# Sums over a head's features: one product with a block-diagonal matrix in place of sums by token, a copy and transposes

## The chip, the cores and the metric

The kernel runs on one core of a Trainium2 chip, as one launch. The time is device microseconds of that core; of the kernel before, three runs are shown. The core has five engines with a program each: TensorE (PE, its weight loads shown as PEld), the vector engine (DVE), the scalar engine (ACT), GpSimd (POOL) and SyncE (SP, which issues the DMAs). They meet at semaphores only.

## What is computed

One inference step through two layers of a hybrid backbone, for 128 context tokens and 256 latent tokens of 1024 features. Each layer is a half-step gated feed-forward, a mixer, and a second half-step feed-forward, each with a layer norm behind it. The mixer's input projection feeds three branches: windowed attention (A), neighbourhood attention (B) and a bidirectional RWKV-7 recurrence (C); each is projected, gated and merged. The change is in branch C, eight heads of 64 features, in two places:

```python
kk = split_heads((k * lp['k_k']).astype(f32), C_HEADS)
kk = kk / jnp.maximum(jnp.sqrt(jnp.sum(kk * kk, axis=-1, keepdims=True)), 1e-12)
...
mu = y.mean(-1, keepdims=True)
var = jnp.mean(jnp.square(y - mu), -1, keepdims=True)
yn = ((y - mu) * lax.rsqrt(var + GN_EPS)).reshape(B, L, C_WIDTH) * lp['gn_g'] + lp['gn_b']
```

Both are a sum over the 64 features of a head for each token, a root, a reciprocal, and a product with each of the 64 features.

## The kernel before

All activations lie with 128 features on the partitions and the 384 tokens along the free axis; a tile of branch C holds two heads (a pair), on partitions 0 to 63 and 64 to 127. Matrix products are made of three float32r products (lines 387 to 389 and 397 to 399) of a high and a low part of weights and activations. The large weights come as a stream of 512 KB units; ACT writes the high part (hi) and DVE the low part (lo). Instructions of ACT, DVE and POOL are recorded through a helper, so all of theirs carry line 290.

The mixer of a layer (`mixer`, line 844) is an attention stage (`attention`, line 1089) and then a scan stage. In the attention stage, `conv_gen` (line 1254) also makes the projections of branch C that the first pairs need, with a convolution over three neighbouring tokens. For a key tile it squares the keys and, two steps into the next projection, runs `norms` (line 1282): the sums kss, a root, a maximum and a reciprocal into rn.

The scan stage (`rwkv_gen`, line 1367) takes four pairs p = 0 to 3 through `rwkv_prepare` (line 1411; the factors of the recurrence, among them nkk, the negated normed keys), `rwkv_chunks` (line 1484; the inversion of 64 x 64 blocks, which begins with products into lu) and `rwkv_scan` (line 1655; the recurrence, then y's group norm with the products gm and gss, then och and ocl, the two parts of the branch's output). The preparation of pair p + 1 and the scan of pair p - 1 are dealt out among the steps of pair p's inversion. Behind the last pair's scan stand the products of branch C's projection (pp<-och).

A small sum is made by `head_sums` (line 1303): the squares serve as weights, 128 tokens at a time, against a constant "sel" of two columns, so the sums come out with tokens on the partitions, six columns (three blocks of tokens, two heads). To bring the six columns of reciprocals back to features on partitions, `head_spread` (line 1308) copies them into a 128 x 384 tile rb, each repeated 64 times, and transposes it block by block into a PSUM tile "spread".

The order is set by a list scheduler from priorities that the program states (`tc.high_priority`, with offsets by stage), and by `beside` (line 1325): every small product or transpose of a scan that goes through `rmm` or `rtr` (lines 1335 and 1339) adds to a debt, by its size and a rate of the phase, and as long as the debt is positive, steps of dense work are issued behind it. That dense work (`mixer_fill`, line 944) is branch B's gates and projections, the projections of the later pairs and branch C's gates (tile pz); what is left of it comes behind the last scan. PSUM tiles come from pools of 3 buffers (kss, pz, pp, among others) and of 2 buffers (spread, gss, gm, up and others of the scan). A constant "blk", 128 x 128 with ones where two features belong to the same head, is there already, for another sum (bon).

Of the kernel before, what the change touches and what calls it, by code (L numbers as in the profile page):

```python
# [101 lines left out]
def _consts():  # L102
# [15 lines left out]
    add("sel", (p[:, None] // HD == np.arange(2)[None, :]))  # L118
# [73 lines left out]
# sets of four groups of 256 modulations; the first two are what the first chunks of features need, then the others  # L192
# [3 lines left out]
def _layout(inp):  # L196
    """Rearranges the inputs (permutations and concatenations only)."""
# [36 lines left out]
    # [l][d][h = (p, e)][v][k] -> [l][(e, k)][p][d][v]  # L234
# [8 lines left out]
def _weights(inp, order):  # L243
    """The large weights as 128 x 128 blocks in the order of their use."""
# [22 lines left out]
def _unlayout(r):  # L267
# [7 lines left out]
    st = r["o_st"].reshape(DEPTH, 2, HD, 4, 2, HD)  # l, e, k, p, d, v  # L275
# [4 lines left out]
class Engine:  # L280
    """An engine that knows its last instruction."""
# [14 lines left out]
def trunk(tc, I, O, order, taps=None, stop=None):  # L296
# [5 lines left out]
    def then(*engines):  # L302
        """Behind the last instruction so far of these engines."""
        st = ExitStack()
        for e in engines or (V, S, G):
            if e.last is not None:
                st.enter_context(tc.issue_after(e.last.ins))
        return st
# [32 lines left out]
    class Stream:  # L341
# [16 lines left out]
        def ahead(self):  # L358
            """Out of the steady state: the unit after the next is split as soon as the last is used up."""
            if len(self.left) <= UNIT and self.unit < WS_UNITS:  # L360
                self.fetch(self.offset)
# [20 lines left out]
    def mm3(out, chunks, xs, after=()):  # L382
        """out += sum of W_k^T x_k, with both factors as sums of two float32r parts."""
# [7 lines left out]
    def mm3_steps(out, chunks, xs, step=2):  # L391
        """mm3 in steps of a few chunks, with what each costs."""
# [10 lines left out]
    def split(dst_h, dst_l, src, lo_eng):  # L403
        """src (SBUF or PSUM, float32) = dst_h + dst_l."""
# [30 lines left out]
    def ada_beside(pool, n):  # L435
        """The next n steps with the products on the vector engine: where that has time, and the tensor engine has not."""
# [38 lines left out]
    def ada_flush():  # L475
        """To columns: out[feature, (block, group, stream)]."""
# [20 lines left out]
    ax = [act.tile([P, NTOK], F32, name=f"ax{c}") for c in range(KD)]  # L497
    # (four more columns: see Norm)
# [8 lines left out]
    class Norm:  # L507
        """Layer norm over the features of y = alpha x + gate * out, chunk by chunk as out comes.
        The next phase's input is h = rs g1 (y - mu) + b1, g1 and b1 per feature and stream, rs and mu per token. Its
        first products W^T h run on z = g1 y, before rs and mu are known: rs W^T z - rs mu W^T g1 + W^T b1, with g1 and  # L510
        b1 as four more columns of z."""
# [34 lines left out]
        def add(self, c, po):  # L546
# [4 lines left out]
            if c == 0:  # L551
                # the table of Sqrt is there when it is needed
# [27 lines left out]
        def pilot(self):  # L580
            # about the mean of the first four chunks
# [14 lines left out]
        def products(self, chunks, xs, c):  # L596
            """The products of chunk c of out."""
# [14 lines left out]
        def finish(self, head=iter(())):  # L612
            """head: products of the next phase, in steps, from those on z to the last before h is needed."""
# [47 lines left out]
        def h(self, pool, c):  # L661
            """The next phase's input, in two parts."""
# [11 lines left out]
        def x(self):  # L674
            """alpha times the norm's output."""
# [5 lines left out]
    class Head:  # L681
        """The first products of a phase, on z: two groups of them, each chunk by chunk."""
# [1108 lines left out]
```

## Time and profile before

| | |
|---|---|
| median of 3 runs | 2436.55 us (2436.5 to 2436.74) |
| span of the profiled execution | 2439.6 us (the profile gives no other time of that execution) |
| instructions | 42863 |
| PE busy | 2297.4 us, 94% of the span |
| PEld busy | 2106.5 us, 86% |
| DVE busy | 1696.6 us, 70% |
| ACT busy | 1056.4 us, 43% |
| POOL busy | 550.0 us, 23% |
| chain that ended last | PE 71%, DVE 15%, ACT 5%, issue 4%, DMA 3%, POOL 2% |
| mean granted TensorE clock | 0.983 |

The profile is of one execution, by the hardware profiler. Busy time is the union of an engine's instructions; a matmul's end is modelled, so that neighbouring matmuls overlap in it, and what a product costs is read from the distance of the starts. The chain is followed back from the last instruction, at each step to what released it. In the window tables each engine's busy time stands with its count of instructions, and PEclk is the clock that the throttle granted TensorE, as a share of full speed.

### The profile page before, as it was taken

How to read it: one execution, taken by the hardware profiler on the slowest of the kernel's cores; microseconds unless marked ns; L12 is line 12 of the kernel's file. 1: busy time of each engine (PE TensorE's matmuls, PEld its weight loads, DVE VectorE, ACT ScalarE, POOL GpSimd, SP SyncE). 2: the span in 40 equal slices, each digit the busy share in tenths (PEclk: the TensorE clock that was granted, in tenths of full speed). 3: DMA queues.
4: the chain of work that ended last, by engine and by line, in shares of the span. 5: the costliest groups of instructions: out<-in, count | busy, mean ns of one | idle time of the engine just before them, and what ended most of it. 6: DMA issues, size and time to landing. Idle time of an engine off the chain costs nothing.

```text
span 2439.6 us, 42863 instructions
## 1 busy us (share of the span) xinstructions
PE 2297.4 (94%) x17066; PEld 2106.5 (86%) x17066; DVE 1696.6 (70%) x2865; ACT 1056.4 (43%) x1942; POOL 550.0 (23%) x522
## 2 busy tenths in 40 slices
PE   7999999998899998999999999899989999999998
PEld 5999988897777788999889999889877777889997
DVE  3797886777767568786978954776787674665534
ACT  3333245655545445333243332555555454443332
POOL 2111422101122044211432113310022220542113
PEclk9999999999999999999999999999999999999999
DMA  8575644242111262665546743523321113534332
GB/s 314 193 240 198 191 122 130 84 111 78 40 57 47 72 209 95 191 217 180 180 147 205 244 130 122 154 81 91 112 70 39 51 50 90 204 102 140 130 121 87
DMA packets 125079, 324.54 MB, mean 133 GB/s; under 512 B 31568, under 2 KB 50256, under 8 KB 124880
## 3 DMA queue, kind: packets, MB, share of 16 engines
q1 hardware_dynamic: 124880, 321.81, 41.1%
q8 instruction: 134, 2.20, 0.4%
q14 instruction: 65, 0.53, 0.1%
HBM read 312.06 MB, written 9.70 MB: 132 GB/s over the span
## 4 chain that ended last, share of the span: by engine, by line
PE 71%; DVE 15%; ACT 5%; issue 4%; DMA 3%; POOL 2%; SPq 0%; POOLq 0%; ACTq 0%; DVEq 0%
PE po L399 5%; PE po L398 5%; PE po L397 5%; PE pa L387 4%; PE pg L389 4%; PE pa L388 4%; PE pg L387 4%; PE pg L388 4%; PE pa L389 4%; DVE lo L290 3%; DVE acc L290 2%; PE pz L397 2%; DMA adaw<-wada 2%; ACT hi L290 2%; PE pz L398 2%
## 5 line engine op out<-in xcount | busy, mean ns | idle before, releaser
L290 DVE TENSOR_TENSOR lo<-raw,hi 128x1024 fp32r<-128x1024 f32 (+1 forms) x472 | 583.8, 1246 | 305.9 <-ACT hi L290 303.8
L290 ACT ACTIVATE hi<-raw 128x1024 fp32r<-128x1024 f32 x418 | 441.7, 1058 | 785.0 <-issue 267.5
L290 DVE SCALAR_TENSOR_TENSOR acc<-adaw,cs,acc 128x1024 f32<-128x1024 f32 x224 | 292.3, 1327 | 0.0
L290 POOL TENSOR_TENSOR ul<-si,uh 128x384 fp32r<-128x384 f32 x88 | 126.3, 1435 | 579.3 <-ACT uh L290 579.3
L399 PE MATMUL po<-uh,lo 128*128 128x384 f32 x704 | 238.6, 339 | 6.3 <-DVE lo L290 6.3
L397 PE MATMUL po<-uh,hi 128*128 128x384 f32 x704 | 239.7, 340 | 0.0
L398 PE MATMUL po<-ul,hi 128*128 128x384 f32 x704 | 238.0, 338 | 0.0
L387 PE MATMUL pg<-zh,hi 128*128 128x384 f32 x656 | 224.1, 342 | 9.1 <-DVE si L290 9.1
L388 PE MATMUL pg<-zl,hi 128*128 128x384 f32 x656 | 223.8, 341 | 0.0
L389 PE MATMUL pg<-zh,lo 128*128 128x384 f32 x656 | 223.2, 340 | 0.0
L387 PE MATMUL pa<-zh,hi 128*128 128x384 f32 x632 | 216.2, 342 | 4.9 <-ACT si L290 4.4
L389 PE MATMUL pa<-zh,lo 128*128 128x384 f32 x632 | 213.8, 338 | 0.6 <-DVE lo L290 0.6
L388 PE MATMUL pa<-zl,hi 128*128 128x384 f32 x632 | 214.2, 339 | 0.0
L399 PEld LDWEIGHTS po<-uh,lo 128*128 128x128 f32 x704 | 133.5, 190 | 7.3 <-DVE lo L290 7.3
L397 PE MATMUL pz<-zh,hi 128*128 128x384 f32 x352 | 128.1, 364 | 8.5 <-ACT hi L290 5.7
L397 PEld LDWEIGHTS po<-uh,hi 128*128 128x128 f32 x704 | 133.7, 190 | 2.2 <-issue 0.8
L398 PEld LDWEIGHTS po<-ul,hi 128*128 128x128 f32 x704 | 133.5, 190 | 1.4 <-issue 0.8
L387 PEld LDWEIGHTS pg<-zh,hi 128*128 128x128 f32 x656 | 125.0, 191 | 10.0 <-ACT hi L290 6.7
L399 PE MATMUL pz<-zh,lo 128*128 128x384 f32 x352 | 126.3, 359 | 4.1 <-DVE lo L290 4.0
L387 PEld LDWEIGHTS pa<-zh,hi 128*128 128x128 f32 x632 | 119.1, 188 | 9.8 <-ACT si L290 5.3
L389 PEld LDWEIGHTS pg<-zh,lo 128*128 128x128 f32 x656 | 125.6, 191 | 1.6 <-issue 1.6
L388 PEld LDWEIGHTS pg<-zl,hi 128*128 128x128 f32 x656 | 125.0, 191 | 1.6 <-issue 1.6
(390 smaller groups left out, 5157.4 us busy)
## 6 DMA issues: line engine op xcount, KB each, us to landing
raw<-ws SPq DMA_DIRECT2D x418, 512.0 KB, 3.5
adaw<-wada SPq DMA_DIRECT2D x144, 512.0 KB, 4.8
bm<-rpb SPq DMA_DIRECT2D x64, 64.0 KB, 7.1
axd<-ax SPq DMA_DIRECT2D x16, 192.0 KB, 5.2
gcd<-gt SPq DMA_DIRECT2D x16, 192.0 KB, 4.7
gc<-gcd SPq DMA_DIRECT2D x16, 192.0 KB, 3.4
ax<-axd SPq DMA_DIRECT2D x16, 192.0 KB, 4.8
xt<-xt SPq DMA_DIRECT2D x8, 192.0 KB, 8.6
```

The costliest lines, as they stand in the source:

```text
L290: self.last = f(*a, **k)
L387: T.matmul(out, wh, xh, start=(k == 0), stop=False)
L388: T.matmul(out, wh, xl, start=False, stop=False)
L389: T.matmul(out, wl, xh, start=False, stop=(k == n - 1))
L397: T.matmul(out, wh, xh, start=(k == 0), stop=False)
L398: T.matmul(out, wh, xl, start=False, stop=False)
L399: T.matmul(out, wl, xh, start=False, stop=(k == n - 1))
```

## The change

The constant "sel", `head_sums` and `head_spread` go. Each sum is one product of the block-diagonal constant "blk" with the 128 x 384 squares, whose result stands on every feature of the head at once; root and reciprocal run on all of it. For the keys, the minus sign goes into the maximum's instruction, rn is a tile of 128 x 384 (two buffers), and the normed keys are one instruction in its place. For the group norm, root and reciprocal overwrite the tile of the squares (gsq). The sum of the group norm now goes through `rmm`, and the transposes, which went through `rtr`, are gone.

```diff
-    add("sel", (p[:, None] // HD == np.arange(2)[None, :]))
...
                 def norms(p=p, sq=sq):
                     pss = mmp("kss")
-                    head_sums(pss, sq)
-                    w[f"rn{p}"] = rn = keep.tile([P, 6], F32, name=f"rn{p}")
-                    S.activation(out=rn, in_=pss[:, 0:6], func=AF.Sqrt)
-                    V.tensor_scalar(out=rn, in0=rn, scalar1=1e-12, scalar2=None, op0=ALU.max)
+                    T.matmul(pss[:, :NTOK], C("blk"), sq, start=True, stop=True)
+                    w[f"rn{p}"] = rn = keep.tile([P, NTOK], F32, tag="rn", bufs=2, name=f"rn{p}")
+                    S.activation(out=rn, in_=pss[:, :NTOK], func=AF.Sqrt)
+                    V.tensor_scalar(out=rn, in0=rn, scalar1=1e-12, scalar2=-1.0, op0=ALU.max, op1=ALU.mult)
                     V.reciprocal(rn, rn)
...
-    def head_sums(out, sq):
-        for b in range(3):
-            T.matmul(out[:, 2 * b : 2 * b + 2], sq[:, b * P : (b + 1) * P], C("sel"), start=True, stop=True)
-
-    def head_spread(pool, rn):
-        rb = pool.tile([P, 3, 2, HD], F32, tag="rb", bufs=1, name="rb")
-        V.tensor_copy(rb, rn.rearrange("p (b e) -> p b e", e=2).unsqueeze(3).to_broadcast([P, 3, 2, HD]))
-        pe = rwp("spread")
-        for b in range(3):
-            rtr(pe[:, b * P : (b + 1) * P], rb[:, b].rearrange("p e f -> p (e f)"))
-        return pe[:, :NTOK]
...
-        nkk = pool.tile([P, NTOK], F32, tag="nkk", bufs=1, name="nkk")
-        V.tensor_scalar(out=nkk, in0=k, scalar1=vcol(l, "k_k")[:, p : p + 1], scalar2=-1.0, op0=ALU.mult, op1=ALU.mult)
-        V.tensor_tensor(out=nkk, in0=nkk, in1=head_spread(pool, w[f"rn{p}"]), op=ALU.mult)
+        nkk = w[f"rn{p}"]
+        V.scalar_tensor_tensor(out=nkk, in0=k, scalar=vcol(l, "k_k")[:, p : p + 1], in1=nkk, op0=ALU.mult, op1=ALU.mult)
...
         pst = rwp("gss")
-        head_sums(pst, sq)
-        rn = pool.tile([P, 6], F32, tag="grn", bufs=1, name="grn")
-        S.activation(out=rn, in_=pst[:, 0:6], func=AF.Sqrt, bias=C("geps"), scale=1.0 / HD)
-        V.reciprocal(rn, rn)
-        V.tensor_tensor(out=k, in0=k, in1=head_spread(pool, rn), op=ALU.mult)
+        rmm(pst[:, :NTOK], C("blk"), sq, start=True, stop=True)
+        S.activation(out=sq, in_=pst[:, :NTOK], func=AF.Sqrt, bias=C("geps"), scale=1.0 / HD)
+        V.reciprocal(sq, sq)
+        V.tensor_tensor(out=k, in0=k, in1=sq, op=ALU.mult)
```

Since priorities and the debt of dense work set the order, the edit moves other instructions too. The rows below are of the instruction order of the two kernels; the number behind a name tells one buffer's contents from the next, and lines from 290 on are lower in the changed kernel.

The vector engine in the attention stage, at the second kss of the first layer (nm, sm and pe are the softmax's maximum, sum and probabilities; lo the low part of a weight unit; r a projection with its convolution). Before:

```order
L290 TENSOR_REDUCE nm<-sl 128x1 x2
L290 TENSOR_SCALAR nm<-nm 128x2
L290 TENSOR_SCALAR rn_5337<-rn_5337 128x6
L290 RECIPROCAL rn_5337<-rn_5337 128x6
L290 TENSOR_TENSOR lo<-raw,hi 128x512 x2
L290 RECIPROCAL sm<-sm 128x2
L290 TENSOR_SCALAR pe<-pe,sm 128x384 x2
```

Now:

```order
L289 TENSOR_REDUCE nm<-sl 128x1 x2
L289 TENSOR_SCALAR nm<-nm 128x2
L289 TENSOR_SCALAR rn_5333<-rn_5333 128x384
L289 RECIPROCAL rn_5333<-rn_5333 128x384
L289 TENSOR_TENSOR lo<-raw,hi 128x512 x2
L289 RECIPROCAL sm<-sm 128x2
L289 SCALAR_TENSOR_TENSOR r_5379<-pc,vec_108,r_5379 128x127
L289 TENSOR_SCALAR pe<-pe,sm 128x384 x2
```

The wide maximum and reciprocal stand at the place of the narrow ones, ahead of the same softmax, and one product of a convolution has come ahead of the probabilities.

The vector engine at the end of the first layer's last scan (k holds y, gp the norm's gain, gc the gates of branch C). Before:

```order
L290 TENSOR_TENSOR k_6257<-gm,gp 128x384
L290 RECIPROCAL grn<-grn 128x6
L290 COPY rb<-grn 128x384
L290 TENSOR_TENSOR lo<-raw,hi 128x1024
L290 TENSOR_TENSOR k_6257<-k_6257,spread 128x384
L290 SCALAR_TENSOR_TENSOR gc<-gc,pp 128x384 x2
```

Now:

```order
L289 TENSOR_TENSOR k_6245<-gm,gp 128x384
L289 RECIPROCAL gsq<-gsq 128x384
L289 TENSOR_TENSOR lo<-raw,hi 128x512
L289 TENSOR_TENSOR k_6245<-k_6245,gsq 128x384
L289 TENSOR_TENSOR lo<-raw,hi 128x512 x7
L289 TENSOR_TENSOR lo<-raw,hi 128x1024 x2
L289 SCALAR_TENSOR_TENSOR gc<-gc,pp 128x384
```

Copy and spread are gone, and seven and two low parts of weights now stand between the norm's product and the first use of branch C's projection.

TensorE at the same place: the gss of the last pair and what follows it (pz is a gate's product, pp<-och and pp<-ocl branch C's projection). Before:

```order
L1306 MATMUL gss<-con,gsq 128x2 x3
L399 MATMUL pz<-zh_95,lo 128x384
L397 MATMUL pz<-zh_97,hi 128x384
L398 MATMUL pz<-zl_98,hi 128x384
L399 MATMUL pz<-zh_97,lo 128x384
L397 MATMUL pz<-zh_99,hi 128x384
L398 MATMUL pz<-zl_100,hi 128x384
L399 MATMUL pz<-zh_99,lo 128x384
L397 MATMUL pz<-zh_101,hi 128x384
L398 MATMUL pz<-zl_102,hi 128x384
L399 MATMUL pz<-zh_101,lo 128x384
L397 MATMUL pp<-och_6919,hi 128x384
```

Now, the last rows ahead of the first pp<-och:

```order
L396 MATMUL pz<-zh_101,hi 128x384
L397 MATMUL pz<-zl_102,hi 128x384
L398 MATMUL pz<-zh_101,lo 128x384
L396 MATMUL pp<-och_6878,hi 128x384
L397 MATMUL pp<-ocl_6879,hi 128x384
L396 MATMUL pp<-och_6878,hi 128x384
```

Before, 10 dense products stand between the last gss and the first product on och; now 134, all of them gates' products. Counted over the first layer's scan stage, up to the last gss, 125 dense products fewer stand on TensorE. Between the first lu of one pair and of the next there are 20 more (pair 0 to 1), 64 fewer (1 to 2) and 39 fewer (2 to 3), and from there to the last gss 39 fewer. Loads of ACT's function tables in its order are 44 where there were 40.

## Rows read from the trace of the kernel before

**Rows 1.** Windows, first layer's scans: engines' busy time (instructions), clock, DMA share, GB/s

```profile
575.00:890.00 315.00, 291.33 (x3575) 243.17 (x3573) 221.82 (x453) 156.07 (x286) 72.15 (x97) 0.98 0.23 74
```

**Rows 2.** Windows, cut at each pair's first lu and at the last gss

```profile
605.00:659.96 54.96, 48.34 (x712) 40.06 (x712) 40.23 (x78) 30.42 (x59) 12.13 (x20) 0.94 0.12 41
659.96:734.00 74.04, 70.66 (x884) 58.52 (x884) 51.76 (x118) 34.20 (x67) 15.24 (x22) 0.98 0.18 56
734.00:793.90 59.90, 56.85 (x812) 46.15 (x810) 45.22 (x95) 32.35 (x63) 14.95 (x21) 0.97 0.15 48
793.90:866.00 72.10, 66.42 (x894) 55.20 (x893) 41.94 (x99) 33.06 (x59) 6.71 (x7) 1.00 0.23 72
```

**Rows 3.** Windows, 30 us and 5 us of the first pair's section

```profile
600.00:630.00 30.00, 25.79 (x362) 23.15 (x362) 26.42 (x49) 14.55 (x27) 4.04 (x5) 0.90 0.17 54
...
625.00:630.00 5.00, 4.69 (x107) 4.68 (x108) 2.30 (x7) 3.08 (x4) 0.00 (x0) 0.50 0.01 3
```

**Rows 4.** TensorE's waits, 575 to 890 us: total us, times, longest us

```profile
PE spread L1340 <- ACT gp L290: 1.5, 2, 0.8
...
PE pp L398 <- POOL ocl L290: 0.5, 1, 0.5
...
PE pp L397 <- ACT och L290: 0.3, 1, 0.3
```

**Rows 5.** Timeline of TensorE, last pair: start, us, instruction

```profile
864.44 0.83 PE L1306 MATMUL gss<-con,gsq 128*128 128x2 f32 x6
...
867.49 0.34 PE L397 MATMUL pp<-och,hi 128*128 128x384 f32 x1
867.67 0.49 PE L1340 MATMUL spread<-con,rb 128*128 128x128 f32 x3
867.91 0.42 PE L398 MATMUL pp<-ocl,hi 128*128 128x384 f32 x1
868.17 0.34 PE L399 MATMUL pp<-och,lo 128*128 128x384 f32 x1
868.35 0.34 PE L397 MATMUL pp<-och,hi 128*128 128x384 f32 x1
```

**Rows 6.** Timeline of TensorE, bonus sum of the last pair

```profile
799.41 0.81 PE L1336 MATMUL bon<-bo,con 128*128 128x384 f32 x2
```

**Rows 7.** Groups by line and shape, vector engine: reciprocals

```profile
L290 DVE RECIPROCAL sm<-sm 128x2 f32<-128x2 f32 x48 | 7.8, 162 | 15.0 <-ACT pe L290 14.6
...
L290 DVE RECIPROCAL rn<-rn 128x6 f32<-128x6 f32 x8 | 1.5, 188 | 0.2
...
L290 DVE RECIPROCAL rs<-dd 128x3 f32<-128x3 f32 x6 | 1.0, 170 | 0.0
```

**Rows 8.** Tile nkk: durations ns min/median/max, first and last start

```profile
L290 DVE TENSOR_SCALAR nkk<-k,vec x8: 401/408/561, 575.0 to 1900.1; 128x384 f32<-128x384 f32 x8
L290 DVE TENSOR_TENSOR nkk<-nkk,spread x8: 541/545/555, 578.7 to 1945.8; 128x384 f32<-128x384 f32 x8
```

**Rows 9.** Timeline of the vector engine at the second kss

```profile
566.47 0.17 DVE L290 TENSOR_SCALAR rn<-rn 128x6 f32<-128x6 f32 x1 [1.44 <-ACT rn L290]
566.68 0.19 DVE L290 RECIPROCAL rn<-rn 128x6 f32<-128x6 f32 x1
567.43 1.29 DVE L290 TENSOR_TENSOR lo<-raw,hi 128x512 fp32r<-128x512 f32 x2 [0.56 <-ACT hi L290]
569.98 0.17 DVE L290 RECIPROCAL sm<-sm 128x2 f32<-128x2 f32 x1 [1.25 <-ACT pe L290]
```

**Rows 10.** Tile rb

```profile
L290 DVE COPY rb<-rn x8: 335/352/403, 575.4 to 1925.6; 128x384 f32<-128x384 f32 x8
```

**Rows 11.** Tile gsq

```profile
L290 ACT ACTIVATE gsq<-gm x8: 472/490/492, 707.5 to 2065.7; 128x384 f32<-128x384 f32 x8
```

**Rows 12.** Groups by line and shape, scalar engine: table loads

```profile
L290 ACT ACT_TABLE_LOAD x40 | 51.3, 1283 | 20.7 <-DMA gcd<-gt 9.3 <-PE pz L398 4.4 <-DMA axd<-ax 4.0
```

**Rows 13.** Timeline of the vector engine, a short convolution

```profile
578.42 0.34 DVE L290 SCALAR_TENSOR_TENSOR v<-pc,vec,v 128x127 f32<-128x127 f32 x1
```

## The prediction

> **What bounds the kernel now.** I read the stretches first, since a share of busy time over the whole span mixes phases. The two sums that change stand in the mixer: the root for a pair's keys (the tile rn, from kss) late in the attention and beside the scans, the group norm (gss) at the end of each pair's scan. In the scan stage of the first layer [rows 1] TensorE is busy 291.33 of 315 us, the vector engine 221.82, the scalar engine 156.07. The reader is to see that TensorE sets the time and stands idle for only 23.7 us, so a change can act in two ways: on TensorE's work, or on those idle pieces. Cut at the first product of each pair's inversion (lu) [rows 2], the three full sections take 54.96, 74.04 and 59.90 us, 188.9 together, with TensorE busy 48.34, 70.66 and 56.85 (175.85, so 13.05 idle) and the vector engine 40.23, 51.76 and 45.22 (137.21, a share of 0.726; the highest section has 0.755). From the last pair's lu on the vector engine has room (41.94 of 72.10), so I take no loss there. Where the vector engine gets denser, TensorE loses: from 600 to 630 us [rows 3] the vector engine has 26.42 of 30, and TensorE only 25.79. The list of TensorE's waits [rows 4] says which of them the change touches: 1.5 us behind the spread, and 0.3 and 0.5 us for och and ocl of the last pair. The median of the runs shown is 2436.55 us; the profiled span is 2439.6, 3.05 us (0.13%) above it. Terms are worked out in the span and added to the median; 0.2%, about what a measurement of this kernel can tell from no change, is 4.9 us.
>
> **Part 1, TensorE's own work.** Sixteen sites (four pairs, two layers, kss and gss) lose three transposes each. At the last pair [rows 5] the start before them is 867.49 and the start four products on is 868.35: 0.86 us, of which the dense products, 0.175 apart, account for three steps or 0.525. So the three cost 0.34 us; at the most the 0.49 that they are shown as. The order shows most of them apart from each other among dense products, so I take 0.45: **16 x 0.45 = -7.2 us** (-5.4 to -7.8). The sums cost the same as before: six records of two columns are busy 0.83 us [rows 5], a product of the same shape as the new one (bon, 384 columns) 0.81 [rows 6]. Zero.
>
> **Part 2, the vector engine.** Each site swaps a reciprocal over 6 columns for one over 384, of which the trace has none. Its rows [rows 7] give 162 ns for 2 columns, 170 for 3 and 188 for 6: 6.5 ns a column between the ends, 8 between the first two. A reciprocal as cheap as any other 384-column operation would be 0.41 to 0.55 us [rows 8]; by the rows' own slope it is 162 + 382 x 6.5 = 2.65 us, by the steeper step 3.2. I take 2.65, since only these rows show the operation itself, and the longest baseline is the surest. A kss site then pays 2.65 - 0.19 for the reciprocal and 0.41 - 0.17 for the wider maximum [rows 8, 9], saves the copy (0.35 [rows 10]) and the product with k_k (0.41), and keeps one product of 0.55: 2.46 + 0.24 - 0.35 - 0.41 = +1.94. A gss site pays 2.46 and saves the copy: +2.11. Eight of each: +32 us on the vector engine, none of it time by itself.
>
> **Part 3, the scalar engine.** Roots over 384 columns instead of 6 cost at the most the 0.49 us of the square of that shape [rows 11], 7.8 us in all, and the order counts 44 loads of its tables instead of 40, at 1283 ns [rows 12] 5.1 us. That engine is idle half of the stage [rows 1]; zero, with both as bounds. The same holds for the tile gsq, held until the norm is done, and rn with two buffers: the vector engine comes to them in its own order, behind the reciprocal costed below.
>
> **Part 4, the end of the scans.** The order moves 125 dense products a layer, 21.8 us of TensorE's work, from beside the scans to behind the last gss. There 134 stand between it and the first product on och, 23 us by 0.175; before there were ten. The last chain is 2.65 us of reciprocal and five steps (root, product, POOL's sum, two for the split) of about half a microsecond [rows 8, 11], some 5 us, so the waits for och and ocl [rows 4] go: 0.8 x 2 = **-1.6 us**.
>
> **Part 5, the attention.** The second kss stands ahead of a softmax on the vector engine. Its reciprocal and maximum make 2.70 us more. What lies between has slack [rows 9]: idle 0.56 before the split and 1.25 before the softmax's reciprocal, 1.81 in all. A 128x127 product that now stands ahead adds 0.34 [rows 13]. So the probabilities come 2.70 - 1.81 + 0.34, about 1.2 us late, and the order has TensorE's transposes of them next. The first kss has more slack; I give it 0.5. **2 x 1.7 = +3.4 us** (from 0, if TensorE has other work then, to 10.8, if all four pay 2.70).
>
> **Part 6, the scan sections.** This is the largest term and the least certain. Removed transposes no longer drip dense products, so sections change by +20, -64 and -39 of them. TensorE's work becomes 48.34 + 3.50 - 0.45, 70.66 - 11.20 - 0.90 and 56.85 - 6.83 - 0.90 = 51.4, 58.6 and 49.1, together 159.1. The vector engine's, with what the order moves there at the prices above, becomes 45.4, 50.2 and 43.6, together 139.2: its share of TensorE's work goes from 0.78 to 0.87. What share of the time it then reaches decides. At the old mean of 0.726 the sections would take 191.7 us, at the highest old section's 0.755 184.4, at 0.88 as in [rows 3] it would not matter at all. But in that piece TensorE reached 25.79 of 30, 0.86: two engines that wait for each other don't both fill. I take 0.78, just above the highest section, which leaves TensorE 0.89: 139.2 / 0.78 = 178.5 us, 19.4 idle instead of 13.05. **2 x 6.35 = +12.7 us** (at 0.755 +24.6, at 0.82 -4.7). That the sections shrink from 188.9 is no gain; the work comes back behind the scans.
>
> **Sum:** -7.2 - 1.6 + 3.4 + 12.7 = +7.3, so 2443.9 us. By the bounds of part 6 it runs from 2426 to 2456.
>
> **The rivals.**
> *Faster.* The reciprocals lie wholly under TensorE's work. Then the transposes, the waits for och and ocl and those at the spread (1.5 x 2 [rows 4]) go, and half of part 5 stays: -7.2 - 1.6 - 3.0 + 1.7 = -10.1, 2426.5 us. For it: TensorE is busy 93% of the stage, and the chain from kss to the scaled keys loses a round trip over TensorE. Against: the cover is what the change takes out of these sections.
> *No change.* The vector engine reaches 0.80: 139.2 / 0.80 = 174.0, 14.9 idle, +3.7 in two layers; -7.2 - 1.6 + 3.4 + 3.7 = -1.7, 2434.9 us. The choice between 0.78 and 0.80 is fine, hence its chance.
> *A dearer reciprocal.* At 3.2 us, six of the eight in a layer fall into the three sections: 6 x 0.55 / 0.78 = 4.2 us more a layer, 8.5 in all, 2452 us. It decides if the steeper step holds. The Trainium skill, page "VectorE: DVE Perf Modes", section "First, the fixed hardware budget", says that a reciprocal is an iterative divide with a repeat count of 8. An estimate from that and the page's clock of 0.96 GHz is 8 x 384 / 0.96 = 3.2 us, by which the sum would be this rival's. The trace agrees only in so far as its rows give 6.5 to 8 ns a column.
> *Cover too thin for the clock.* From 625 to 630 us TensorE ran at a granted clock of 0.50 [rows 3], the lower of its two levels, 1.2 GHz, at the end of the 30 us in which the vector engine had 26.42; 4.69 us busy at half speed lose 2.35. If two pairs in each layer, with 64 and 39 products less, each add one such piece, 4 x 2.35 = 9.4 come on top of the forecast: 2453 us. Against: granted clocks of 0.97 and 0.98 in these very sections [rows 2].
> That the change doesn't do what it says can be left out: the order shows the transposes gone and the wide reciprocals in place.
>
> **How the numbers follow.** Forecast 0.33 (its own range 2439 to 2448), faster 0.25, no change 0.27, dearer reciprocal 0.10, clock 0.05. The range from 2426 to 2456 leaves out half of the faster case and a little of the last two, under 0.2. Faster by over 0.2% is below 2431.7: the faster case, 0.25. Within 0.2%: no change and a tenth of the forecast, 0.30. Slower, above 2441.4: the rest, 0.45.
>
> **What would show it.** A reciprocal of 128x384 near 2.65 us (part 2); no wait of TensorE for spread, och or ocl, and some 130 dense products behind the last gss (parts 1 and 4); TensorE waiting for the probabilities after the second kss about 1 us longer (part 5); in the three sections about 19 us of TensorE's idle time instead of 13, ended by the vector engine (part 6). The prediction is wrong if the reciprocal is under a microsecond, or if idle time in these sections does not grow though the vector engine's work does.

## The result, and the profile after

Over seven runs of either kernel the changed one took 2452.03 us (2448.75 to 2460.96) where the one before took 2440.31 (2436.5 to 2448.19): a ratio of 1.0053, with a 95% interval of 1.0037 to 1.0069. It is slower by half a per cent; on the 2436.55 us of the forecast that is 2449.5. The profiled execution of the changed kernel took 2458.35 us, with a span of 2456.6, 17.0 more than that of before.

The head of its page:

```profile
span 2456.6 us, 42603 instructions
...
PE 2315.7 (94%) x16954; PEld 2116.6 (86%) x16954; DVE 1712.1 (70%) x2841; ACT 1067.2 (43%) x1946; POOL 551.1 (22%) x522
```

TensorE's busy time is 18.3 us longer than the 2297.4 of before, although its work is less, and its idle time is the same (140.9 us of the span, 142.2 before). The mean granted clock fell from 0.983 to 0.971. At the lower level a product takes nearly twice as long: the output product's dense products of 384 columns start 0.32 us apart at 0.50 (893.69, 894.01, 894.33 us) and 0.175 apart at 1.00 (896.91, 897.08, 897.26). So time at that level is lost by half at the most: 0.029 x 2456.6 = 71.2 us in this execution, 0.017 x 2439.6 = 41.5 before. The difference, 29.7 us, is a bound for these two executions, of which the changed kernel's is the second slowest of its seven. Over all seven its mean clock is 0.974, where the kernel before has 0.982 in its 17 executions beside the first experiments: at the most 0.008 x 2440 = 20 us, for 13 measured. Among the seven alone the span grows by 12.2 us from the clock of 0.977 to that of 0.968; at that rate 0.008 is some 11 us. The clock can thus be most of the loss, but there are gains and other losses beside it, as the stretches show.

Groups by line and shape, the reciprocals and the table loads (answering to [rows 7, 12]; us in all, mean ns, then idle time before them):

```profile
L289 DVE RECIPROCAL rn<-rn 128x384 f32<-128x384 f32 x8 | 20.4, 2554 | 0.3
L289 DVE RECIPROCAL gsq<-gsq 128x384 f32<-128x384 f32 x8 | 20.4, 2550 | 5.4 <-ACT gsq L289 5.4
...
L289 ACT ACT_TABLE_LOAD x44 | 56.5, 1283 | 7.2 <-DMA cc<-cc 2.6 <-DMA axd<-ax 2.1 <-PE pz L398 1.7
```

The windows of the first layer, cut at the second kss, at each first lu (a transpose on the vector engine, not a product; each inversion begins with it), at the last gss and around the output product (engines in the order of [rows 1], then granted clock, DMA share, GB/s). Kernel before, the two stretches that [rows 2] do not have:

```profile
564.80:605.00 40.20, 34.40 (x203) 28.23 (x202) 30.06 (x58) 22.05 (x39) 11.50 (x20) 1.00 0.23 68
886.40:924.70 38.30, 35.41 (x195) 33.39 (x195) 24.77 (x34) 16.16 (x26) 19.55 (x17) 1.00 0.58 198
```

Changed kernel, from the second kss to the last gss, and the output product:

```profile
564.90:609.70 44.80, 38.77 (x197) 32.00 (x196) 30.11 (x55) 22.45 (x39) 11.04 (x20) 0.85 0.23 71
609.70:667.20 57.50, 52.10 (x722) 42.29 (x722) 44.42 (x82) 31.96 (x61) 12.31 (x20) 0.94 0.12 41
667.20:731.40 64.20, 61.17 (x819) 48.21 (x819) 51.58 (x106) 35.80 (x67) 14.69 (x22) 0.97 0.15 49
731.40:781.60 50.20, 47.39 (x753) 36.76 (x754) 44.22 (x90) 29.47 (x58) 15.40 (x19) 1.00 0.11 35
781.60:837.20 55.60, 53.29 (x832) 44.89 (x830) 38.30 (x96) 29.41 (x55) 7.42 (x9) 1.00 0.18 57
882.80:927.40 44.60, 38.41 (x195) 35.28 (x194) 25.16 (x36) 16.89 (x27) 21.49 (x18) 0.96 0.36 117
```

Three things are to be seen. From the second kss to the first inversion the stretch is 4.6 us longer with the same idle time (6.03 us, 5.80 before), at a clock of 0.85 instead of 1.00. The sections of the pairs, where the largest loss was forecast, are shorter (57.5, 64.2 and 50.2 us), and TensorE is idle there for 11.2 us instead of 13.05. And the output product takes 44.6 us instead of 38.3. In the second layer the first of these comes again (44.5 us at 0.85), the three sections go from 187.1 to 180.5 us with 11.3 us idle instead of 12.5, and the clock falls to 0.81 between the first two inversions (64.5 us, 55.1 before).

TensorE's timeline shows what stands ahead of the low clock. Kernel before (start, us, instruction, in brackets the wait and what ended it):

```profile
570.38 0.65 PE L1067 MATMUL po<-ptl,vt 128*64 128x256 f32 x2 [1.82 <-ACT ptl L290]
570.95 0.87 PE L987 MATMUL pt<-con,pe 128*128 128x128 f32 x6
...
594.29 0.87 PE L1340 MATMUL pb<-con,bk 128*128 128x128 f32 x6 [1.31 <-POOL bk L290]
```

Changed kernel, and its windows behind each wait:

```profile
572.21 1.51 PE L986 MATMUL pt<-con,pe 128*128 128x128 f32 x6 [2.95 <-DVE pe L289]
...
597.43 0.87 PE L1325 MATMUL pb<-con,bk 128*128 128x128 f32 x6 [2.43 <-POOL bk L289]
...
572.00:578.00 6.00, 5.21 (x19) 3.32 (x20) 2.55 (x7) 1.75 (x4) 0.59 (x3) 0.50 0.27 90
...
600.00:606.00 6.00, 6.00 (x23) 5.46 (x22) 4.49 (x8) 1.06 (x1) 3.69 (x5) 0.50 0.04 11
```

The probabilities (pe) came late, as forecast: their transposes (pt) start at 572.21 where they started at 570.95, and TensorE waited for them 2.95 us in one piece, where it had waited 1.82 for something else, with two products (po) between. For POOL's factors (bk) it waited 2.43 us instead of 1.31. Behind both waits of the changed kernel the granted clock is 0.50, its lower level of 1.2 GHz, for 6 us; behind those of the kernel before it stays at 1.00.

The 0.81 of the second layer stands behind such a wait too, for the transposed inverse (yr). The kernel before has that wait as well, and behind it the clock was at the lower level for some 7 us; here it was for 20. Second layer, kernel before and then changed:

```profile
1827.06 0.98 PE L1336 MATMUL pz<-yr,gt 16*32 16x16 f32 x96 [2.44 <-DVE yr L290]
...
1829.10:1835.90 6.80, 6.56 (x143) 6.03 (x145) 2.51 (x8) 3.13 (x4) 0.00 (x0) 0.50 0.01 2
```
```profile
1834.66 1.42 PE L1321 MATMUL pz<-yr,gt 16*32 16x16 f32 x96 [2.69 <-DVE yr L289]
...
1834.80:1855.20 20.40, 20.05 (x318) 14.00 (x311) 10.96 (x19) 9.42 (x15) 0.31 (x2) 0.50 0.14 49
```

At the output product TensorE waits for the last high parts (mh) of the merge:

```profile
PE po L396 <- ACT mh L289: 3.4, 2, 2.4
...
876.01 0.56 DVE L289 SCALAR_TENSOR_TENSOR ml<-ax,mh 128x384 fp32r<-128x384 f32 x1 [1.68 <-ACT mh L289]
876.49 0.55 DVE L289 SCALAR_TENSOR_TENSOR gc<-gc,pp 128x384 f32<-128x384 f32 x1
...
879.64 0.56 DVE L289 SCALAR_TENSOR_TENSOR ml<-ax,mh 128x384 fp32r<-128x384 f32 x1 [1.46 <-ACT mh L289]
880.11 0.55 DVE L289 SCALAR_TENSOR_TENSOR gc<-gc,pp 128x384 f32<-128x384 f32 x1
```

On the vector engine a gate's product (gc) and a low part (ml) now take turns, each ml idle until ACT's high part, which waits for POOL, which waits for the gc before. One round takes 2.7 or 3.6 us; before, they went by twos, and two rounds together took 4.7 us (877.80 to 882.47). From the first product on och to the end of the output product, both layers, kernel before and then changed:

```profile
867.00:924.90 57.90, 53.40 (x294) 50.40 (x293) 38.60 (x49) 26.12 (x39) 29.73 (x25) 1.00 0.66 223
2068.80:2129.60 60.80, 55.34 (x295) 52.07 (x295) 38.76 (x49) 26.18 (x40) 29.79 (x25) 0.97 0.62 212
```
```profile
864.10:927.60 63.50, 56.35 (x292) 52.14 (x292) 35.21 (x49) 23.76 (x38) 28.59 (x23) 0.97 0.49 161
2082.60:2146.10 63.50, 56.33 (x291) 52.11 (x291) 35.20 (x49) 23.76 (x37) 28.56 (x23) 0.97 0.47 153
```

With the products the same, that is 5.6 and 2.7 us more.

### The profile page after: what moved, and what is told of

Its sections match the earlier page's. It is cut to its first block, busy times and chain, and to the rows that moved or that the text cites. A ratio compares the mean times of both kernels' runs of the same rounds, so it can differ in the third digit from the quotient of the medians.

```text
span 2456.6 us, 42603 instructions
## 1 busy us (share of the span) xinstructions
PE 2315.7 (94%) x16954; PEld 2116.6 (86%) x16954; DVE 1712.1 (70%) x2841; ACT 1067.2 (43%) x1946; POOL 551.1 (22%) x522
## 5 line engine op out<-in xcount | busy, mean ns | idle before, releaser
L289 DVE TENSOR_TENSOR lo<-raw,hi 128x1024 fp32r<-128x1024 f32 (+1 forms) x472 | 574.2, 1226 | 335.2 <-ACT hi L289 333.7
L397 PE MATMUL pz<-zl,hi 128*128 128x384 f32 x352 | 127.2, 362 | 0.0
```

What stands on the lines that cost most here:

```text
L289: self.last = f(*a, **k)
L397: T.matmul(out, wh, xl, start=False, stop=False)
```

## The experiments

All ratios are to the kernel before on the same chip, with a 95% interval; a difference of two kernels is one of two such ratios. Three theories were on trial. **W**: long waits of TensorE, behind which its clock falls. **L**: the load of the vector engine beside the scans, as forecast in part 6. **M**: the merge's new order.

### One half at a time

The first takes `norms` and nkk of the change and keeps the group norm, whose copy goes into the tile of the squares for want of room:

```diff
-        rb = pool.tile([P, 3, 2, HD], F32, tag="rb", bufs=1, name="rb")
+        rb = rb.rearrange("p (b e f) -> p b e f", b=3, e=2)
...
-        V.tensor_tensor(out=k, in0=k, in1=head_spread(pool, rn), op=ALU.mult)
+        V.tensor_tensor(out=k, in0=k, in1=head_spread(sq, rn), op=ALU.mult)
```

The second takes the group norm of the change alone, word for word.

> Only the keys' sums are changed; the group norm is as before (its copy goes into the tile of the squares). Theory W (the wait behind the second kss, and TensorE's granted clock falling to its lower level right after it): the wide reciprocal still stands ahead of a softmax, so from the second kss to the first inversion the time is 4 us or more longer than before in each layer, with a granted clock near 0.85 there, and the whole is slower by 0.3 to 0.6%. Theory L (load of the vector engine beside the scans): half of the load is gone, so about half of the loss, +0.2 to 0.3%, and it lies in the three sections of the pairs. Theory M (the merge's products in another order at the end): the order still alternates gates and low parts one by one, so 3 us or more idle in the output product of each layer.

Measured: 1.0120 (1.0100 to 1.0141).

> Only the group norm is changed; the keys' sums are as before. Theory W: the second kss costs what it did, clock 1.00 there, so the whole is within 0.2% of before. Theory L: half of the load and half of the loss, +0.2 to 0.3%, as idle time in the sections. Theory M: the merge goes by twos and threes again, so its idle time goes back to under 4 us in each layer.

Measured: 1.0034 (1.0018 to 1.0050). The stretch behind the second kss and the output product of each, and a section of the keys' half; the keys' half first, then the norm's:

```profile
566.00:610.60 44.60, 38.63 (x196) 31.75 (x195) 29.64 (x55) 22.47 (x39) 11.01 (x20) 0.85 0.23 71
732.60:787.30 54.70, 52.84 (x750) 41.74 (x750) 37.97 (x89) 30.96 (x59) 12.38 (x19) 0.88 0.10 32
892.60:938.40 45.80, 39.74 (x196) 36.59 (x195) 25.30 (x36) 17.03 (x27) 21.68 (x18) 0.93 0.37 119
```
```profile
564.80:605.00 40.20, 34.37 (x203) 28.19 (x203) 30.07 (x58) 22.07 (x39) 11.51 (x20) 1.00 0.21 68
891.10:931.00 39.90, 36.21 (x196) 33.33 (x196) 25.20 (x35) 16.69 (x27) 18.64 (x17) 1.00 0.61 207
```

The place is that of W: 44.6 us at 0.85 with the keys' half, 40.2 at 1.00 without it. M's place is right too: 45.8 us of output product with the keys' half, 6 of them idle, 39.9 with the other, whose merge goes by twos and threes. But the sizes were missed. The keys' half alone is dearer than the whole change: its second row, the section between the last two inversions, is at a clock of 0.88 where the whole change has 1.00. The low piece in it lasts 13.6 us, and TensorE's longest wait in the 18 us ahead of it is 0.7 us, so here the clock fell without a long wait, and W does not explain it:

```profile
754.60:768.20 13.60, 13.60 (x159) 11.54 (x161) 6.12 (x14) 5.17 (x10) 2.85 (x6) 0.50 0.20 75
```

The second layer has such a piece too. The norm's half was to be free by W and was not; L's size for it (0.2 to 0.3%) lies in the interval. Its twelve executions have a mean clock of 0.980, the kernel before 0.982, so the clock is at the most 4 of its 8 us. Where the extra time lies its one profile, of a span no longer than that of before (2438.7 us), does not show.

### The reciprocals left out

```diff
-                    V.reciprocal(rn, rn)
+                    V.tensor_scalar(out=rn, in0=rn, scalar1=-0.05, scalar2=-0.05, op0=ALU.max, op1=ALU.min)
...
-        V.reciprocal(sq, sq)
+        V.tensor_scalar(out=sq, in0=sq, scalar1=0.5, scalar2=0.5, op0=ALU.max, op1=ALU.min)
```

> The changed kernel with each of the 16 wide reciprocals replaced by a clamp to a constant: the reciprocals are left out. Each then takes about 0.36 us instead of 2.55, all else is as in the change. Theory W: the wait for the probabilities is as short as before or shorter and the clock stays at 1.00, so 8 us or more of the 13 come back, 2441 or less on the chip of before. Theory L: the same direction, but the gain lies in the sections of the pairs, 6 us a layer, and the clock is as in the changed kernel. Theory M: at most 4 us come back, since the merge still alternates.

Measured: 1.0052 (1.0032 to 1.0071), the same as with the reciprocals. W and L had both forecast a gain; only M's "at most 4 us" has room for this. The vector engine has 35 us less to do, and nothing is gained beyond the 6 us or so that the two intervals could hide, so L falls in the size that was forecast. The order is nearly, not quite, the same: 12 more dense products stand behind the last gss. The wait stays long without the reciprocal as well:

```profile
572.22 0.85 PE L986 MATMUL pt<-con,pe 128*128 128x128 f32 x6 [2.32 <-DVE pe L289]
...
596.24 0.88 PE L1325 MATMUL pb<-con,bk 128*128 128x128 f32 x6 [2.40 <-POOL bk L289]
...
566.14 1.28 ACT L289 ACT_TABLE_LOAD   x1
567.44 0.49 ACT L289 ACTIVATE rn<-kss 128x384 f32<-128x384 f32 x1
...
568.89 1.28 ACT L289 ACT_TABLE_LOAD   x1
570.19 0.58 ACT L289 ACTIVATE pe<-sl,nm 128x384 f32<-128x384 f32 x1
```

What makes the softmax late is not only the reciprocal. On ACT the root over 384 columns (0.49 us for 0.18) and the load of its table stand ahead of the table and the exponentials of the same softmax, now behind two copies (ptl) instead of one: from the start of the second kss on TensorE to the first pe on ACT there are 4.63 us here (565.56 to 570.19) and in the change (564.92 to 569.55), and 3.94 before (564.77 to 568.71).

### Later, by priority

```diff
-                    V.tensor_scalar(out=rn, in0=rn, scalar1=1e-12, scalar2=-1.0, op0=ALU.max, op1=ALU.mult)
-                    V.reciprocal(rn, rn)
+                    if p != 1:
+                        V.tensor_scalar(out=rn, in0=rn, scalar1=1e-12, scalar2=-1.0, op0=ALU.max, op1=ALU.mult)
+                        V.reciprocal(rn, rn)
...
+        if p == 1:
+            V.tensor_scalar(out=nkk, in0=nkk, scalar1=1e-12, scalar2=-1.0, op0=ALU.max, op1=ALU.mult)
+            V.reciprocal(nkk, nkk)
```

> The changed kernel, with maximum and reciprocal of the second pair's keys (the second kss) moved to the start of that pair's preparation, beside the first pair's inversion. The vector engine does the same work. Theory W: from the second kss to the first inversion as before, 40 us instead of 44.5 in each layer, clock 0.97 or more, 8 us in all against the changed kernel, so about +0.2% against before. Theory L: no gain, or a loss of 1 to 3 us, since more of the load is in the sections. Theory M: nothing changes in the output product.

Measured: 1.0168 (1.0146 to 1.0191). The edit did not do what it meant: preparation has a higher priority, and the scheduler put both instructions back to where they were (the reciprocal at 567.74, TensorE's wait for pe again 2.95 us). It did bring 73 dense products a layer back from behind the scans, and in the first layer the last two sections went from 50.2 and 55.6 us to 60.9 and 65.7. It tells nothing of W.

### The wait cut into pieces

```diff
                     V.reciprocal(rn, rn)
+                    if p == 1:
+                        for _ in range(2):
+                            T.matmul(pss[:, :NTOK], C("blk"), rn, start=True, stop=True)
```

> The changed kernel with two products of 384 columns more on TensorE in each layer, whose results nobody reads: they read the reciprocal of the second kss, and stand between the products and the transposes among which TensorE waited 2.95 us for the probabilities. The rest of the order is the same. The chain of the softmax stays as late as it is; only the wait is cut into pieces of about 1 and 0.6 us with 1.3 us of work between. Theory W (the granted clock falls behind a long wait, and that is what costs): clock 1.00 behind it, from the second kss to the first inversion about 41.5 us instead of 44.5 in each layer, 6 us in all, so about 1.003 of the time of before. If the lateness of the chain itself were the loss: no gain, 1.005 as the changed kernel, or a little more.

Measured: 1.0012 (0.9999 to 1.0024). Useless work on TensorE makes the kernel 0.4% faster than the change:

```profile
570.50 1.53 PE L1290 MATMUL kss<-rn,con 128*128 128x384 f32 x4 [1.16 <-DVE rn L289]
572.29 0.85 PE L986 MATMUL pt<-con,pe 128*128 128x128 f32 x6 [0.26 <-DVE pe L289]
...
594.83 1.46 PE L1328 MATMUL pb<-con,bk 128*128 128x128 f32 x6 [2.10 <-POOL bk L289]
...
566.00:596.00 30.00, 25.59 (x131) 20.28 (x130) 21.77 (x40) 18.13 (x32) 6.79 (x13) 0.98 0.27 86
596.00:602.00 6.00, 6.00 (x29) 5.33 (x28) 4.03 (x8) 1.37 (x3) 2.21 (x4) 0.50 0.05 15
```

The transposes start at 572.29, as late as in the change (572.21), but the wait is 1.16 and 0.26 us, and the clock is 0.98 over the 30 us in which it had been at 0.50 for six. It falls only behind the second wait, which was left (2.10 us). In this layer the stretch took 43.7 us. In the second layer that wait, again 2.10 us, had no low clock behind it, and the stretch took 40.0 us, where the change had 44.5. No other instruction changes its place on any engine. So lateness by itself is not the loss; the clock behind the long wait is.

### The merge by twos

```diff
-                for m in range(KD):
+                for m0 in range(0, KD, 2):
+                    for m in (m0, m0 + 1):
...
+                    behind = V.last.ins
...
+                        with tc.issue_after(behind):
                             V.scalar_tensor_tensor(out=ml, in0=ax[m], scalar=0.5, in1=mh.bitcast(F32), op0=ALU.mult, op1=ALU.subtract)
```

> The changed kernel with the merge of branch C dealt out by twos again: the two gates' products of two chunks on the vector engine, then the two low parts, as in the kernel before. Nothing else moves. Theory M: the wait of 2.4 us for the last high part goes, and with it the piece at the lower clock behind it: 5 us or more in each layer at the output product, 8 to 10 in all, so 1.001 to 1.002 of the time of before. If the alternation is hidden: 1.005 as the changed kernel.

Measured: 0.9983 (0.9967 to 0.9998): 0.7% off the change by the order in which 16 instructions a layer take turns; all others keep their places. From the first product on och to the end of the output product, both layers, to be held against 63.5 us each:

```profile
871.60:928.50 56.90, 53.82 (x291) 50.84 (x291) 36.68 (x49) 23.58 (x38) 25.35 (x23) 1.00 0.54 178
2070.30:2128.00 57.70, 53.78 (x291) 50.84 (x292) 36.77 (x49) 23.53 (x38) 25.36 (x23) 1.00 0.55 179
```

M stands, and is larger than expected (about 17 us for 8 to 10). The two profiles place 12.4 us of it here (6.6 and 5.8); the rest is not placed by one profile of each. Most of the 12.4 is idle time and not the clock: of the 63.5 us TensorE was idle for 7.2, of 56.9 and 57.7 for 3.1 and 3.9, and the clock (0.97 for 1.00) is at the most 1.9 us a layer. Over all executions the mean clock is 0.976 here and 0.974 in the change, at the most 5 of the 17 us.

### Both repairs

> Both of the two kernels above together. If W and M are two separate losses they add up: 14 us less than the changed kernel, 0.998 to 1.000 of the time of before. If either only shifts the loss to a later wait, it stays above 1.002.

Measured: 0.9973 (0.9956 to 0.9989). They do not add up in full (0.4 and 0.7% off the change one by one, 0.8% together), but this is the version that beats both kernels: the change, two idle products a layer, and the merge by twos.

> As the one before, and two such products more in each layer for the second long wait (2.4 us, for POOL's factors of the first pair). They also shift dense products from behind the scans back beside them (73 of 136 in the first layer). Theory W: no piece at the lower clock between the second kss and the first inversion, another 3 us a layer, 0.995 to 0.998 of the time of before. If where the dense products stand is what counts, and not the clock: a loss against the one before, since the last two sections grow by what comes back.

Measured: 1.0017 (1.0004 to 1.0031). The second wait is cut, the stretch behind the second kss is at 0.96 and 1.00 in the two layers (41.3 and 40.4 us), and yet the kernel is slower. The rival named there holds: 73 dense products came back beside the scans. From the first inversion to the first product on och in the two layers, with both repairs, and with the second cut as well:

```profile
609.30:864.10 254.80, 240.18 (x3260) 196.79 (x3259) 187.47 (x381) 137.20 (x251) 52.09 (x72) 0.97 0.20 66
1802.30:2060.40 258.10, 241.43 (x3260) 197.77 (x3260) 187.52 (x381) 137.39 (x251) 52.08 (x72) 0.97 0.20 66
```
```profile
605.30:873.00 267.70, 251.67 (x3268) 204.41 (x3267) 187.99 (x382) 137.00 (x251) 52.14 (x72) 0.95 0.17 56
1812.00:2078.20 266.20, 248.67 (x3269) 202.58 (x3268) 188.27 (x382) 136.90 (x251) 52.50 (x72) 0.96 0.18 57
```

The vector engine does the same there, and TensorE the same but for a handful of records; yet the stretch is 12.9 and 8.1 us longer. Idle time is 1.4 and 0.9 of it, the clock (0.02 and 0.01 lower) some 5 and 3; for the rest TensorE was busy longer over the same products. Why is not shown. That the change moves 125 dense products from beside the scans to behind them looks by this like a gain, which the forecast did not have. The two layers of the change do not show it alike: in the first this stretch takes 254.4 us where it took 262.0 before, in the second 265.7 where it took 259.5, at a clock of 0.94 instead of 0.98. By the lengths of the pieces at 0.50 the clock costs there at the most 5.1 and 17.1 us, before 6.8 and 5.1; without them the stretch would be some 6 us shorter than before in either layer.

> The kernel with both repairs (one cut wait, the merge by twos), and the second long wait cut too, without moving anything else: two products of 384 columns more in each layer, whose result nobody reads, on the keys' factors (kd) of the first pair, which POOL has ready about 0.9 us into TensorE's wait of 2.1 us for bk. Theory W: the clock is 1.00 from the second kss to the first inversion in both layers, 41 us or less in each, and the whole is 0.9955 to 0.997 of the time of before. If the earlier try on this wait was slower because it was cut, and not because dense products came back beside the scans: 1.000 or more.

Measured: 0.9973 (0.9959 to 0.9987), the same as with one cut wait. The edit missed its aim: POOL's factors kd came 2.28 us into the wait, not 0.9, so that it stayed long. In the first layer no low clock followed, in the second 0.72 over 6 us.

### The old kernel made late, and its own wait cut

Both start from the kernel before; first `norms`, then the first pair's `rwkv_chunks`:

```diff
                     V.reciprocal(rn, rn)
+                    if p == 1:
+                        V.tensor_scalar(out=sq, in0=sq, scalar1=rn[:, 0:1], scalar2=None, op0=ALU.mult)
+                        V.reciprocal(sq, sq)
...
         pz = atp("pz1")
+        if p == 0:
+            for _ in range(1):
+                T.matmul(pz[:, :NTOK], C("ident"), ty.rearrange("p a b -> p (a b)")[:, :NTOK], start=True, stop=True)
```

> The kernel before, with two instructions more on the vector engine in each layer, whose results nobody reads: behind the reciprocal of the second kss a product and a reciprocal over 384 columns (0.41 and 2.55 us), ahead of the softmax, as the change has them; sums, copy and transposes are as before. By the slack of 1.81 us there the probabilities come 1.15 us later. Theory W: TensorE waits about 2.9 us in one piece instead of 1.82, the granted clock falls behind it, and 3 to 4.5 us are lost in each layer: 1.0025 to 1.004 of the time of before. If a microsecond of lateness is absorbed, or costs only itself: 1.000 to 1.001.

Measured: 1.0021 (1.0007 to 1.0034), some 5 us, a little under W's range, with TensorE's order unchanged. Here the wait came in two pieces, since the products between (po) still stand ahead of it on TensorE:

```profile
570.56 0.65 PE L1067 MATMUL po<-ptl,vt 128*64 128x256 f32 x2 [1.82 <-ACT ptl L290]
572.10 0.85 PE L987 MATMUL pt<-con,pe 128*128 128x128 f32 x6 [0.89 <-DVE pe L290]
...
574.00:576.00 2.00, 2.00 (x10) 0.93 (x6) 0.00 (x0) 0.00 (x0) 0.00 (x0) 0.50 0.09 35
```

In the first layer the clock fell behind them, in the second (1.82 and 0.89 us as well) it did not. The old kernel can be brought into part of the same loss by lateness alone; that this part is the clock is not shown as clearly (mean clock of the twelve executions 0.980, before 0.9815, at the most 4 of the 5 us).

> The kernel before, with one product of 384 columns more on TensorE in each layer, whose result is overwritten: it stands in the wait of 2.44 us for the first pair's transposed inverse (yr), behind which the granted clock was 0.50 to 0.67. Theory W: the clock stays at 1.00 there, the section from the first inversion to the second shrinks by 2.5 to 3.5 us in each layer, 0.997 to 0.999 of the time of before: the mechanism was in the old kernel too. If the low clock there has another cause than the wait: 1.000 or a little more.

Measured: 1.0068 (1.0048 to 1.0087). A miss: the tile it reads was ready only at the end of the wait, so that the wait was 2.57 us in one piece instead of 2.44 and the product came on top. The product also moved the order: 14 of 89 dense products left the section from one pair's yr to the next pair's, 18 more stand between the third and the fourth, and instructions of the vector engine changed places. So it is no test of a cut wait. It agrees with W in one thing: the clock behind this wait stayed at the lower level for 20 and 24 us in the two layers, where it had been for 7.

```profile
1836.60:1860.40 23.80, 23.80 (x360) 18.57 (x360) 9.53 (x21) 9.35 (x15) 0.31 (x2) 0.50 0.14 46
```

### The reciprocals once more, with the waits repaired

> The kernel with both repairs (the cut wait and the merge by twos), with each of the 16 wide reciprocals replaced by a clamp to a constant: the reciprocals are left out. It tells what 35 us of vector-engine work cost where the long waits they cause are taken out. Theory W: nothing, within 0.2% of the kernel with both repairs, 0.996 to 0.999 of the time of before. Theory L: 10 us or more less, 0.993 or below.

Measured: 0.9951 (0.9934 to 0.9967), 0.22% below the kernel with both repairs, whose interval it overlaps. The 16 wide reciprocals cost 5 us by these two ratios, nothing by the pair above, and not the 10 or more of L.

## Why the prediction was right, and where its steps were not

The sign was right, the size a little small (2443.9 us forecast, 2449.5 by the ratio), and the time lies within the range, by luck: terms that were wrong in both directions cancel. Step by step:

**Part 1** held: transposes and copies are gone; the last pair's group norm sum is busy 0.86 us where it was 0.83. Its price was not measured by itself. **Part 2** held: a reciprocal of 384 columns took 2.55 us for 2.65. The estimate from the Trainium skill ("VectorE: DVE Perf Modes", "First, the fixed hardware budget") had been 3.2 us; the measurement decides: from 188 ns at six columns on it is 6.25 ns a column. The rival of a dearer reciprocal is out. **Part 3** had the work right (44 loads of tables, roots of 0.49 us) and the price of zero wrong, as part 5 shows.

**Part 4** was half right. No wait for och or ocl is left, but the pieces behind the last gss now wait for what is next: the weights' high part, a gate and low parts, 2.7 us up to the end of branch C's projection where there were 1.6. And the forecast had read in the order that low parts of weights stand ahead of the first gc, without reading on: the alternation of gc and ml stands a few rows below. Its price, about 17 us by the ratio without it, was the largest single one.

**Part 5** had the lateness right, 1.1 us against 1.2 (from the start of the second kss to the transposes 7.29 us, before 6.18), though 0.69 of it came by ACT, and its price wrong: 1.7 us a layer were forecast, 4.6 and 4.2 came. Idle time in that stretch is about what it was; the rest is TensorE at half speed behind the waits. The rival of the clock, given 0.05, had this loss but not its cause: it laid the low clock to thin cover, where the piece that it read (625 to 630 us, [rows 3]) begins behind the single wait of 2.44 us for yr.

**Part 6**, the largest term, is the step that failed most: "I take 0.78, just above the highest section". The vector engine's work came as forecast (44.42 + 51.58 + 44.22 = 140.2 us for 139.2), but its share rose to 0.82 over the three sections, and to 0.88 in one, with TensorE at 47.39 of 50.2. Idle time fell to 11.2 us where 19.4 were forecast. That two engines that wait for each other don't both fill was taken from one piece of 30 us [rows 3], and 2.44 of TensorE's 4.21 idle us there are the one wait for yr. Leaving out the reciprocals, which should have given the term back, gave nothing in the change, and with the waits repaired some 5 us, not clear of zero. The prediction's own sign of being wrong, idle time there that does not grow, came.

So the total was right for the wrong reason. By the stretches of the two profiles, both layers together: from the second kss to the first inversion +8.8 us (forecast +3.4); from there to the first product on och -1.4 (forecast +12.7 of load, less 7.2 of transposes, most of which stand here), held up by the second layer's low clock; from there to the end of the output product +8.3 (forecast -1.6). That is 15.7 of the 17.0 us between them. The load did not come; the clock behind the long waits and the merge took its place.

## What to carry to other kernels

Where TensorE is busy nine tenths of the time, ask of each instruction put ahead of a chain not only how late it makes the chain, but how long TensorE's longest single wait becomes, and read the granted clock behind waits of that length elsewhere in the trace; cutting a wait can pay though the chain stays as late. When an edit moves a scheduler's order, read the order of the engines to the end of the phase: the dearest move here was in instructions that the edit doesn't touch. And do not price an engine's share by one stretch in which it was high.

## What the runs showed of the hardware that was not expected

Behind single waits of 2.95 us for pe and 2.43 for bk the granted clock was at its lower level for 6 us; behind those of 1.82 and 1.31 us in the same places of the kernel before, at the upper one. In all five kernels whose profile has the wait for pe in one piece (the change, its half for the keys, the merge by twos, the later maximum, no reciprocals; 2.95 us, in the last 2.32) the clock fell behind it, in both layers. It is not the same each time for shorter ones: behind waits of 2.10 us the clock fell in one layer of one execution and not in the other, behind the 1.82 us it fell in one layer of the old kernel with its own wait cut (0.51 from 1785.4 to 1788.8 us), and the seven runs of the changed kernel, the same instructions each, had spans of 2447.0 to 2459.2 us with mean clocks of 0.977 to 0.968. Why the low clock behind the wait for yr lasts some 3 us in one layer of the change and 20 in the other (0.94 and 0.81 in the section) stays open; no run cut that wait. Also open are the low clock of 13.6 us without a long wait in the keys' half, why dense products cost more beside the scans than behind them, and why the two repairs overlap.
